# Two transformer blocks on one core: matmuls of the up stretches in program order, and the Strassen forms placed behind the norm

## Chip, core and metric

The kernel runs on one core of one Trainium2 chip. The metric is the device time of one execution in microseconds. TensorE is the matrix engine (PE in the profile, PEld its weight loads), VectorE is DVE, ScalarE is ACT, GpSimd is POOL, SyncE is SP, which issues the loads of the weights.

## What is computed

Two blocks of two layers each, in float32, width 1024. The change lies in the second block: 512 tokens and 16 learned ones (528, and 512 in the last stage), and in each of its two layers twice a gated feed-forward net, before and after a mixer.

```python
def swiglu(x, w_gate, w_up, w_down):
    return (jax.nn.silu(x @ w_gate) * (x @ w_up)) @ w_down
...
    for l in range(DEPTH):
        h = h + 0.5 * swiglu(rmsnorm(h, norm_gains[l, 0]),
                             ffn_w_gate[l, 0], ffn_w_up[l, 0], ffn_w_down[l, 0])
        h = h + mixer(rmsnorm(h, norm_gains[l, 1]), w_in[l], ...)
        h = h + 0.5 * swiglu(rmsnorm(h, norm_gains[l, 2]),
                             ffn_w_gate[l, 1], ffn_w_up[l, 1], ffn_w_down[l, 1])
    return rmsnorm(h, final_norm)[:, N_META:]
```

w_gate and w_up are 1024 x 2816, w_down is 2816 x 1024. So the net is run four times, as the stages (0,0), (0,1), (1,0) and (1,1) of layer and place.

## The kernel before

Activations lie with the features on the partitions, as 8 chunks (NK) of 128 features by 528 tokens, `xt`. Every operand of a matmul is split into a high and a low part of a faster float format, and every product is made of three matmuls (high by high, high by low, low by high): `mm3` does so for a chunk of 128 features, in two halves of the tokens, and lines 235 and 243 issue its matmuls. Weights are loaded as raw tiles by SyncE (6 buffers), split by ScalarE into `whi` (line 212) and by VectorE into `wlo` (line 213), 9 buffers each. Activations are split by `xsplit` (lines 286, 287) and `split` (lines 220, 221).

**The feed-forward stage, `ffn2`.** The hidden features are 22 blocks m of 128. For each, gate and up are computed, then `act` makes silu(gate) * up and splits it for the down matmuls. Two ways lead to gate and up. Blocks 0, 3, 7, 11, 15, 18 and 21 (DIRECT) use `group`: 8 chunks by 3 by 2 matmuls for gate and for up each. The others, 13 in stage (0,0) and 15 in each of the others, use `strassen`: the 2 x 2 product of (gate, up) weight halves and token halves in seven products instead of eight. Before blocks 8 and 16 and at the end (ROUNDS) the blocks so far go through `down`, which adds into `xt`.

**The seven products.** `pair` loads the four quarter weights a, b, c, d of a block and makes the sums s1 to s4 from them on VectorE (line 1022). Each product (`prod`) is 12 matmuls at line 1042, of 264 columns (256 in the last stage). Y and X are two halves of one PSUM tile `yx`, Z lies in another, `z`; the pool P has three such tiles. In `strassen`:

- a: Y = a x1; then ScalarE copies Y to `fg` (line 1060)
- b: X = b x2; VectorE adds X to `fg` (line 1058), first yield
- s2: Y += s2 f2; ScalarE copies Y (line 1065), second yield
- s1: Z = s1 f1; s3: Y += s3 f1; ScalarE copies Y to `fu` (line 1071), VectorE adds Z, third yield
- d: Y += d f2, and the multiplications by the norm's factors, fourth yield
- s4: Z += s4 x2, and `act`

`ffn2` interleaves two blocks: a, b of block m; d of m-1; s2 of m; s4 of m-1; s1 and s3 of m. A block's d and s4 that are left when a direct block comes are written behind its first group of matmuls.

**The forms.** f1 and f2 are sums and differences of the halves of the activations, scaled by the norm's gains but not by its root. `form` makes one of the four pairs of chunks: a scaled copy on ScalarE (line 322), four operations on VectorE (lines 319 and 325), and two splits (lines 220, 221). `finish`, called for each chunk k when the stage before has finished it, does `xsplit`, the squares for the norm (`sumsq`, lines 299, 300), and for k of 4 and over one form. The first block's last stage (`out1`) does the same for all four in its own loop ahead of stage (0,0).

**The norm.** `stats` sums squares over partitions on TensorE (ssq, line 336), and the reciprocal root is a chain of small VectorE operations (`rsqrt`, lines 357 to 375); `stats2` broadcasts it with matmuls (bc, line 388) and ScalarE copies it to `rbc` (line 411). In `group` with an r, `stats2` is written after the chunk MID (4) of 8. Block 0 then scales gate and up (`mul_r`, line 417), applies silu (line 1111), multiplies (line 1112), and splits. In stage (0,0) the first five groups (gate and up of block 0, 1 and the gate of block 2) run before the norm's factors are known: their results wait in `gur` tiles (line 1105), the last in PSUM, and `rbc` comes out of the last of these groups.

**What sets the order.** The order of the instructions on each engine is found at compile time, by a planner that lets a free engine take the first instruction of the program's order whose inputs it counts as ready; the chip then runs each engine's queue in that order. The tiles of `slot` come from one pool of 62. The down stretches and the groups of blocks over 0 already stand in the program's order; the stretches of seven products do not, nor does `ending`, which finishes the last chunk of the whole kernel in two halves with norm and output.

Of the kernel before, what the change touches and what calls it, by code (L numbers as in the profile page):

```python
# [22 lines left out]
NX = 512  # L23
NMETA = 16
T2 = NX + NMETA
NK = 8
# [34 lines left out]
class Net:  # L61
    def __init__(self, ctx, tc, d):
        nc = self.nc = tc.nc
        self.tc = tc
        self.d = d
        self.n = 0
        self.xp = ctx.enter_context(tc.tile_pool(name="xp", bufs=1))
        self.cp = ctx.enter_context(tc.tile_pool(name="cp", bufs=1))
        self.sp = ctx.enter_context(tc.tile_pool(name="sp", bufs=NSLOT))
        self.mp = ctx.enter_context(tc.tile_pool(name="mp", bufs=24))  # L70
        self.qp = ctx.enter_context(tc.tile_pool(name="qp", bufs=8))
        self.wp = ctx.enter_context(tc.tile_pool(name="wp", bufs=4))
        self.pstack = ctx.enter_context(ExitStack())
        self.block = 0
        self.filler = iter(())
        self.got = {}
        self.forms = None

        self.cst = self.cp.tile([128, 144], F32, name="cst")
        self.v2 = self.cp.tile([128, 2 * V2 + 8], F32, name="v2")  # L80
        self.v1 = self.slot("v1")
        self.xt = [self.xp.tile([128, T2], F32, name=f"xt{k}") for k in range(NK)]
        nc.scalar.dma_start(self.v1[:, : 2 * V1], d["vec1"])
        nc.gpsimd.dma_start(self.cst, d["cst"])
        nc.scalar.dma_start(self.v2, d["vec2"])
        self.pre = []
        self.ident = self.cst[:, 0:128]
        self.c1024 = self.cst[:, 128:129]
        self.c128 = self.cst[:, 129:130]
        self.hm64 = self.cst[:, 130:132]  # L90
# [124 lines left out]
    def split(self, a, name):  # L215
# [5 lines left out]
        nc.vector.tensor_tensor(out=l[:, :T], in0=a, in1=h[:, :T], op=ALU.subtract)  # L221
        return h, l

    def mm3(self, ps, w, wc, xs, T, first, last, M=128, halves=(0, 1)):


        nc = self.nc
        wh, wl = w
        xh, xl = xs
        whole = T == NX and len(halves) == 2  # L230
        for i, (a, b) in enumerate(((wh, xh), (wh, xl), (wl, xh))):
            st, sp = first and i == 0, last and i == 2
            lh = self.wcol(a, wc, M)
            if whole:
                nc.tensor.matmul(ps[:M, :], lhsT=lh, rhs=b[:, :NX], start=st, stop=sp)  # L235
                continue
            for h in halves:
                c = slice(0, 256) if h == 0 else slice(256, T)
                if T == NX:
                    o = ps[:M, c]  # L240
                else:
                    o = ps[:M, 0, 256:512] if h == 0 else ps[:M, 1, 0 : T - 256]
                nc.tensor.matmul(o, lhsT=lh, rhs=b[:, c], start=st, stop=sp)  # L243

    def outs(self, n, T, name="g", tag=None):

# [55 lines left out]
    def finish(self, k, T, g):  # L302

        c = slice(0, T)
        r = self.xsplit(k, g(k), c)
        self.sumsq(k, self.xt[k][:, c], c)
        if self.forms is not None and k >= NK // 2:
            self.form(k - NK // 2, T, g)
        return r

# [136 lines left out]
    def out1(self, srcs, ks, ins, ys, gcol, next_g, tn):  # L447


        nc = self.nc  # L450
        m0 = NK - len(srcs)
        ws = [[self.wload(s) for s in src] for src in srcs]
        ps = [[self.A("oh") for _ in srcs] for _ in range(2)]
        H = (slice(0, 256), slice(256, NX))
        rb = self.slot("rbp")
        for hf in range(2):
            c = H[hf]
            bl = (2 * hf, 2 * hf + 1)
            for i in range(len(srcs)):
                for n, (wi, col, k) in enumerate(ks):  # L460
                    self.mm3(
                        ps[hf][i], ws[i][wi], col, ins[k], NX, n == 0, n == len(ks) - 1, halves=(hf,)
                    )
                if hf == 0:
                    ys.append(self.slot("y"))
                self.evac_y(m0 + i, ps[hf][i][:, c], c, gcol, ys[m0 + i])
            pss = self.S("ssy")
            self.compact(self.acc, bl, self.c1024, pss)
            r = self.rsqrt(pss, bl, 1)
            bc = self.S("bcy")  # L470
            self.bcast(r, bl, bc)
            nc.scalar.copy(rb[:, c], bc[:, c])
        for hf in range(2):
            c = H[hf]
            cn = slice(256, tn) if hf else c
            if hf == 0:
                xs = []
            for k in range(NK):
                nc.vector.tensor_tensor(out=ys[k][:, c], in0=ys[k][:, c], in1=rb[:, c], op=ALU.mult)
                nc.vector.tensor_tensor(out=self.xt[k][:, c], in0=self.xt[k][:, c], in1=ys[k][:, c], op=ALU.add)  # L480
                if hf == 0:
                    xs.append((self.slot("xh", F32R), self.slot("xl", F32R)))
                self.xsplit(k, next_g(k), cn, xs[k])
                if hf == 1 and self.forms is not None and k >= NK // 2:
                    self.form(k - NK // 2, tn, next_g)
            for k in range(NK):
                self.sumsq(k, self.xt[k][:, cn], cn)
        return xs
# [548 lines left out]
    def prod(self, o, w, xs, c, first):  # L1037

        for k in range(NK // 2):
            l = slice(128 * k, 128 * k + 128)  # L1040
            for i, (a, b) in enumerate(((0, 0), (0, 1), (1, 0))):
                self.nc.tensor.matmul(  # L1042
                    o, lhsT=w[a][:, l], rhs=xs[k][b][:, c], start=first and k == 0 and i == 0,
                    stop=k == NK // 2 - 1 and i == 2, skip_group_check=not first,
                )
# [34 lines left out]
        act(s, u, True)  # L1080
        yield

    def ffn2(self, l, f, xs, next_g, out=None):
        nc, d = self.nc, self.d
        T = NX if (l, f) == (L - 1, 1) else T2
        self.psum(2)
# [33 lines left out]
        def ahead(m):  # L1120

            if m not in wp and seven(m):
                wp[m] = self.pair(srcs[2 * m], srcs[2 * m + 1])

        for m in range(NF):
            ahead(m)
            if seven(m):
                if seven(m + 1) and m + 1 not in ROUNDS:
                    ahead(m + 1)
# [7 lines left out]
            else:  # L1137
                ps = done[2 * m : 2 * m + 2]
                o = 2 * m + len(ps)
                if m == 0 and not ps:  # L1140
                    ps = self.outs(2, T, "gu")
                    r = self.stats(T)
                    rb = self.group(srcs[:2], xs, T, ps, r=r)
                    ps = [p[1] for p in ps]
                for i in range(o, 2 * m + 2):
                    if len(ps) == 2:
# [7 lines left out]
            if m + 1 in ROUNDS:  # L1154
# [16 lines left out]
                if fin and out is not None:  # L1171
                    self.ending(out, self.wload(dsrc(NK - 1)), acts)
                acts.clear()
        return new

    def ending(self, out, ws, acts):
# [554 lines left out]
def tile_model(ctx: ExitStack, tc: tile.TileContext, d, out, stages=ALL):  # L1731
# [18 lines left out]
    for i, s in enumerate(stages):  # L1750
# [16 lines left out]
        elif s[0] == "m2":  # L1767
            xs = net.mixer2(s[1], xs, ng)
        else:
            end = nx[0] == "end"  # L1770
            xs = net.ffn2(s[1], s[2], xs, ng, out if end else None)
            if end:
                break

# [178 lines left out]
```

## Time and profile before

| | us |
|---|---|
| median of 3 runs | 3674.74 (3673.05 to 3675.29) |
| profiled execution, time | 3672.45 |
| profiled execution, span of the trace | 3670.7 |
| TensorE busy | 3543.5 (97%) |
| VectorE busy | 2412.7 (66%) |
| ScalarE busy | 1715.2 (47%) |
| DMA, mean of the 16 engines | 82 GB/s read from and written to memory |

The profiled execution is 2.3 us shorter than the median of the runs, and 1.75 us of its time lie outside the span. The mean granted clock of TensorE was 0.988 of full. In the rows below, the idle time in brackets is that of the engine just before the instruction, with what ended it.

### The profile page before, as it was taken

To read this page: it belongs to the slowest core of one execution; us is meant where nothing else is said; L and a number is where in the kernel's file an instruction comes from. 1 tells how busy PE (TensorE), PEld (TensorE's weight loads), DVE (VectorE), ACT (ScalarE), POOL (GpSimd) and SP (SyncE) were. 2 spreads that over 40 slices of the span, in tenths; PEclk is the share of its full clock that TensorE was granted. 3 is DMA by queue.
4 is the path that set the end of the run, shared out by engine and by line. 5 is a ranking of instruction groups with operands and counts; after the bars stand their busy time and mean duration, and the time that the engine had idled before them with its cause. 6 is when DMAs were issued, how large, how long until landed. Compare 5 with 4: busy or idle time off the path is not lost. (4 is left out here: it accounts for less than half of the span.)

```text
span 3670.7 us, 60668 instructions
## 1 busy us (share of the span) xinstructions
PE 3543.5 (97%) x23303; PEld 3142.0 (86%) x23303; DVE 2412.7 (66%) x4863; ACT 1715.2 (47%) x3219; POOL 44.4 (1%) x184
## 2 busy tenths in 40 slices
PE   8999999999999799999999999998999999999998
PEld 6778888768888799998988999998999987778887
DVE  6778754787864666576546766577666664677765
ACT  3655433365543443344573443354334557444433
POOL 1000000000000000000000000000000000000000
PEclk9999999999999999999999999999999999999999
DMA  4213333212333222331121232333333212223232
GB/s 144 67 50 109 95 93 111 72 50 84 95 94 92 77 81 86 88 105 60 54 62 53 78 100 85 91 89 90 88 95 95 74 56 62 67 78 101 87 100 68
DMA packets 170178, 305.02 MB, mean 83 GB/s; under 512 B 19460, under 2 KB 29732, under 8 KB 169888
## 3 DMA queue, kind: packets, MB, share of 16 engines
q1 hardware_dynamic: 165888, 292.89, 27.1%
q0 software_dynamic: 2560, 6.93, 0.6%
q8 instruction: 183, 3.00, 0.4%
q10 hardware_dynamic: 1440, 1.32, 0.1%
q14 instruction: 107, 0.88, 0.1%
HBM read 298.97 MB, written 2.10 MB: 82 GB/s over the span
## 5 line engine op out<-in xcount | busy, mean ns | idle before, releaser
L212 ACT ACTIVATE whi<-raw 128x512 fp32r<-128x512 f32 (+1 forms) x1078 | 662.8, 619 | 1132.1 <-PE dn L235 187.5
L213 DVE TENSOR_TENSOR wlo<-raw,whi 128x512 fp32r<-128x512 f32 (+1 forms) x1078 | 722.8, 672 | 465.4 <-ACT whi L212 450.6
L235 PE MATMUL up<-xh,wlo 128*128 128x512 f32 x640 | 252.7, 395 | 0.0
L235 PE MATMUL up<-xh,whi 128*128 128x512 f32 x640 | 252.5, 395 | 0.0
L235 PE MATMUL up<-xl,whi 128*128 128x512 f32 x640 | 252.1, 394 | 0.0
L212 ACT ACTIVATE whi<-sum 128x512 fp32r<-128x512 f32 x232 | 145.5, 631 | 216.1 <-PE yx L1042 59.5
L243 PE MATMUL dn<-fah,wlo 128*128 128x256 f32 (+1 forms) x1068 | 218.0, 284 | 0.0
L243 PE MATMUL dn<-fah,whi 128*128 128x256 f32 (+1 forms) x1068 | 217.7, 284 | 0.0
L243 PE MATMUL dn<-fal,whi 128*128 128x256 f32 (+1 forms) x1068 | 217.7, 284 | 0.0
L213 DVE TENSOR_TENSOR wlo<-sum,whi 128x512 fp32r<-128x512 f32 x232 | 158.9, 688 | 57.3 <-ACT whi L212 54.0
L243 PE MATMUL g<-xh,whi 128*128 128x256 f32 (+1 forms) x848 | 185.5, 297 | 2.7 <-ACT ptm L1410 1.5
L243 PE MATMUL g<-xl,whi 128*128 128x256 f32 (+1 forms) x848 | 179.7, 288 | 0.0
L243 PE MATMUL g<-xh,wlo 128*128 128x256 f32 (+1 forms) x848 | 177.9, 287 | 0.0
L243 PE MATMUL gu<-xh,whi 128*128 128x256 f32 (+1 forms) x736 | 154.3, 290 | 14.4 <-ACT gur L1105 12.3
L243 PEld LDWEIGHTS dn<-fah,whi 128*128 128x128 f32 x1068 | 167.7, 188 | 0.0
L243 PEld LDWEIGHTS dn<-fah,wlo 128*128 128x128 f32 x1068 | 167.6, 188 | 0.0
L243 PEld LDWEIGHTS dn<-fal,whi 128*128 128x128 f32 x1068 | 167.5, 188 | 0.0
L1042 PE MATMUL yx<-fvh,whi 128*128 128x264 f32 (+1 forms) x464 | 138.7, 299 | 21.8 <-ACT fu L1071 20.1
L243 PE MATMUL gu<-xl,whi 128*128 128x256 f32 (+1 forms) x736 | 155.9, 288 | 1.2 <-DVE xl L287 1.2
L243 PE MATMUL gu<-xh,wlo 128*128 128x256 f32 (+1 forms) x736 | 155.3, 288 | 0.0
L235 PE MATMUL g<-xh,whi 128*128 128x512 f32 x344 | 146.3, 425 | 7.4 <-ACT xh L286 6.3
L243 PEld LDWEIGHTS g<-xh,whi 128*128 128x128 f32 (+1 forms) x848 | 132.8, 188 | 14.5 <-issue 7.1
(538 smaller groups left out, 9574.2 us busy)
## 6 DMA issues: line engine op xcount, KB each, us to landing
raw<-w_in SPq DMA_DIRECT2D x186, 256.0 KB, 2.8
raw<-w_up SPq DMA_DIRECT2D x176, 256.0 KB, 2.8
raw<-ffn_g SPq DMA_DIRECT2D x176, 256.0 KB, 2.8
raw<-ffn_u SPq DMA_DIRECT2D x176, 256.0 KB, 2.9
raw<-ffn_d SPq DMA_DIRECT2D x160, 256.0 KB, 2.7
raw<-w_down SPq DMA_DIRECT2D x80, 256.0 KB, 2.7
raw<-w_out SPq DMA_DIRECT2D x64, 256.0 KB, 2.7
raw<-w_pab SPq DMA_DIRECT2D x32, 256.0 KB, 2.7
```

The lines of the kernel that those rows point to most:

```text
L212: self.nc.scalar.activation(hi[:, c], raw[:, c], AF.Copy)
L213: self.nc.vector.tensor_tensor(out=lo[:, c], in0=raw[:, c], in1=hi[:, c], op=ALU.subtract)
L235: nc.tensor.matmul(ps[:M, :], lhsT=lh, rhs=b[:, :NX], start=st, stop=sp)
L243: nc.tensor.matmul(o, lhsT=lh, rhs=b[:, c], start=st, stop=sp)
L1042: self.nc.tensor.matmul(o, lhsT=w[a][:, l], rhs=xs[k][b][:, c], start=first and k == 0 and i == 0, stop=k == NK // 2 - 1 and i == 2, skip_ ...
```

## The change

It has two parts.

- A helper `mm` issues a matmul and, while `self.pinned` is set, tells the planner to keep it behind the TensorE instruction written before it (an order on the engine's own queue, no wait on a semaphore). `prod` and `mm3` use it. `pinned` is set in `ffn2` from block 1 to the end of the stage, so seven products, groups, down rounds and `ending` stand in the program's order; block 0 and the other stages do not.
- The last of the four forms (k = 7) is no longer made in `finish`, and `out1` makes none. `ffn2` makes those that are missing, in a function `forms`: in stage (0,0) all four behind the five first groups, ahead of the block loop; in the others the last one behind the group of block 0, whose `stats2` comes before it, and ahead of block 0's `act`. `ffn2` gets the norm's gains `g` for that.

```diff
--- before.py
+++ after.py
@@ -75,6 +75,7 @@
         self.filler = iter(())
         self.got = {}
         self.forms = None
+        self.pinned = False
 
         self.cst = self.cp.tile([128, 144], F32, name="cst")
         self.v2 = self.cp.tile([128, 2 * V2 + 8], F32, name="v2")
@@ -221,10 +222,15 @@
         nc.vector.tensor_tensor(out=l[:, :T], in0=a, in1=h[:, :T], op=ALU.subtract)
         return h, l
 
+    def mm(self, *a, **k):
+
+        i = self.nc.tensor.matmul(*a, **k)
+        if self.pinned:
+            self.tc.keep_in_program_order(i)
+
     def mm3(self, ps, w, wc, xs, T, first, last, M=128, halves=(0, 1)):
 
 
-        nc = self.nc
         wh, wl = w
         xh, xl = xs
         whole = T == NX and len(halves) == 2
@@ -232,7 +238,7 @@
             st, sp = first and i == 0, last and i == 2
             lh = self.wcol(a, wc, M)
             if whole:
-                nc.tensor.matmul(ps[:M, :], lhsT=lh, rhs=b[:, :NX], start=st, stop=sp)
+                self.mm(ps[:M, :], lhsT=lh, rhs=b[:, :NX], start=st, stop=sp)
                 continue
             for h in halves:
                 c = slice(0, 256) if h == 0 else slice(256, T)
@@ -240,7 +246,7 @@
                     o = ps[:M, c]
                 else:
                     o = ps[:M, 0, 256:512] if h == 0 else ps[:M, 1, 0 : T - 256]
-                nc.tensor.matmul(o, lhsT=lh, rhs=b[:, c], start=st, stop=sp)
+                self.mm(o, lhsT=lh, rhs=b[:, c], start=st, stop=sp)
 
     def outs(self, n, T, name="g", tag=None):
 
@@ -304,7 +310,7 @@
         c = slice(0, T)
         r = self.xsplit(k, g(k), c)
         self.sumsq(k, self.xt[k][:, c], c)
-        if self.forms is not None and k >= NK // 2:
+        if self.forms is not None and NK // 2 <= k < NK - 1:
             self.form(k - NK // 2, T, g)
         return r
 
@@ -481,8 +487,6 @@
                 if hf == 0:
                     xs.append((self.slot("xh", F32R), self.slot("xl", F32R)))
                 self.xsplit(k, next_g(k), cn, xs[k])
-                if hf == 1 and self.forms is not None and k >= NK // 2:
-                    self.form(k - NK // 2, tn, next_g)
             for k in range(NK):
                 self.sumsq(k, self.xt[k][:, cn], cn)
         return xs
@@ -1039,7 +1043,7 @@
         for k in range(NK // 2):
             l = slice(128 * k, 128 * k + 128)
             for i, (a, b) in enumerate(((0, 0), (0, 1), (1, 0))):
-                self.nc.tensor.matmul(
+                self.mm(
                     o, lhsT=w[a][:, l], rhs=xs[k][b][:, c], start=first and k == 0 and i == 0,
                     stop=k == NK // 2 - 1 and i == 2, skip_group_check=not first,
                 )
@@ -1080,7 +1084,7 @@
         act(s, u, True)
         yield
 
-    def ffn2(self, l, f, xs, next_g, out=None):
+    def ffn2(self, l, f, xs, g, next_g, out=None):
         nc, d = self.nc, self.d
         T = NX if (l, f) == (L - 1, 1) else T2
         self.psum(2)
@@ -1122,8 +1126,15 @@
             if m not in wp and seven(m):
                 wp[m] = self.pair(srcs[2 * m], srcs[2 * m + 1])
 
+        def forms():
+            for k in range(len(self.forms), NK // 2):
+                self.form(k, T, g)
+
+        if done:
+            forms()
         for m in range(NF):
             ahead(m)
+            self.pinned = m > 0
             if seven(m):
                 if seven(m + 1) and m + 1 not in ROUNDS:
                     ahead(m + 1)
@@ -1141,6 +1152,7 @@
                     ps = self.outs(2, T, "gu")
                     r = self.stats(T)
                     rb = self.group(srcs[:2], xs, T, ps, r=r)
+                    forms()
                     ps = [p[1] for p in ps]
                 for i in range(o, 2 * m + 2):
                     if len(ps) == 2:
@@ -1171,6 +1183,7 @@
                 if fin and out is not None:
                     self.ending(out, self.wload(dsrc(NK - 1)), acts)
                 acts.clear()
+        self.pinned = False
         return new
 
     def ending(self, out, ws, acts):
@@ -1768,7 +1781,7 @@
             xs = net.mixer2(s[1], xs, ng)
         else:
             end = nx[0] == "end"
-            xs = net.ffn2(s[1], s[2], xs, ng, out if end else None)
+            xs = net.ffn2(s[1], s[2], xs, g_of["f2"](*s[1:]), ng, out if end else None)
             if end:
                 break
```

## Rows read from the trace of the kernel before

**Rows 1.** Busy time of TensorE, the page's first part: busy us, share, instructions.
```profile
PE 3543.5 (97%) x23303; PEld 3142.0 (86%) x23303; DVE 2412.7 (66%) x4863; ACT 1715.2 (47%) x3219; POOL 44.4 (1%) x184
```

**Rows 2.** TensorE's waits: engine, tile, line <- releaser: us, times, longest us.
```profile
PE yx L1042 <- ACT fu L1071: 20.1, 35, 0.9
PE yx L1042 <- ACT fg L1065: 14.9, 15, 1.0
...
PE bc L388 <- DVE rs_y L375: 12.0, 6, 5.1
...
PE z L1042 <- DVE fg L417: 4.1, 3, 1.7
...
PE yx L1042 <- ACT fg L1060: 1.8, 2, 0.9
```

**Rows 3.** Timeline of TensorE: start us, us, engine, line, tiles, [idle before <-releaser].
```profile
2110.89 0.39 PE L1042 MATMUL yx<-xh,whi 128*128 128x264 f32 x1 [0.93 <-ACT fg L1060]
...
2113.22 0.39 PE L1042 MATMUL yx<-fvh,whi 128*128 128x264 f32 x1 [0.59 <-DVE fg L1058]
```

**Rows 4.** The same of products s3 and d of a block.
```profile
1326.18 0.39 PE L1042 MATMUL yx<-fuh,whi 128*128 128x264 f32 x1 [1.02 <-ACT fg L1065]
1326.40 0.28 PE L1042 MATMUL yx<-ful,whi 128*128 128x264 f32 x1
...
1327.62 0.28 PE L1042 MATMUL yx<-fuh,wlo 128*128 128x264 f32 x1
1328.77 0.39 PE L1042 MATMUL yx<-fvh,whi 128*128 128x264 f32 x1 [0.87 <-ACT fu L1071]
```

**Rows 5.** Timeline of ScalarE between these two products.
```profile
1327.82 0.63 ACT L212 ACTIVATE whi<-raw 128x512 fp32r<-128x512 f32 x1 [1.69 <-PE yx L1042]
1328.36 0.36 ACT L1071 COPY fu<-yx 128x264 f32<-128x264 f32 x1
```

**Rows 6.** Timeline of ScalarE around the norm ahead of the third such stage.
```profile
2482.25 0.63 ACT L220 ACTIVATE fvh<-tv 128x528 fp32r<-128x528 f32 x1
2482.79 0.73 ACT L286 ACTIVATE xh<-xt,v 128x528 fp32r<-128x528 f32 x1
...
2499.86 0.65 ACT L220 ACTIVATE fah<-fg 128x528 fp32r<-128x528 f32 x1 [0.79 <-DVE fg L1112]
...
2501.88 0.36 ACT L1060 COPY fg<-yx 128x264 f32<-128x264 f32 x1
```

**Rows 7.** Windows, matmuls of line 1042: stretch, us, PE and PEld busy (count), clock.
```profile
1317.50:1348.60 31.10, 28.99 (x228) 28.07 (x228) 1.00 0.32 93
...
1547.20:1566.20 19.00, 18.45 (x144) 17.75 (x144) 1.00 0.28 94
...
sum 522.90, PE 492.79 PEld 474.67; mean PE 24.64 PEld 23.73
```

**Rows 8.** Lines by shape, 1257 to 1282 us: busy us, mean ns, idle.
```profile
L319 DVE SCALAR_TENSOR_TENSOR tv<-xt,v,tu 128x264 f32<-128x264 f32 x4 | 2.0, 489 | 0.0
...
L221 DVE TENSOR_TENSOR fvl<-tv,fvh 128x528 fp32r<-128x528 f32 x4 | 2.8, 702 | 0.0
```

**Rows 9.** Timeline of TensorE at the third such stage's norm.
```profile
2489.41 0.28 PE L1042 MATMUL yx<-xh,wlo 128*128 128x264 f32 x1
2494.84 2.61 PE L388 MATMUL bc<-cst,rs_y 128*128 128x128 f32 x10 [5.14 <-DVE rs_y L375]
```

**Rows 10.** Timeline of TensorE at the first such stage's norm.
```profile
1281.32 0.81 PE L243 MATMUL gu<-xh,whi 128*128 128x256 f32 x2 [12.28 <-ACT gur L1105]
```

**Rows 11.** Windows around it: us, then busy us (count) by engine, clock.
```profile
1257.00:1269.00 12.00, 9.27 (x63) 8.05 (x63) 12.00 (x30) 7.92 (x16) 0.00 (x0) 1.00 0.01 2
...
1281.30:1297.00 15.70, 14.38 (x89) 14.05 (x90) 5.87 (x19) 3.34 (x6) 0.00 (x0) 0.71 0.13 39
```

**Rows 12.** Timeline of VectorE behind that norm.
```profile
1306.82 0.70 DVE L417 TENSOR_TENSOR fg<-gu,rbc 128x528 f32<-128x528 f32 x1
...
1311.90 0.71 DVE L417 TENSOR_TENSOR fg<-gu,rbc 128x528 f32<-128x528 f32 x1 [0.55 <-PE gu L243]
```

## The prediction

> **What bounds the kernel now.** I read the page first, then the waits of TensorE, then the timeline of single places. TensorE is busy 3543.5 of 3670.7 us [rows 1], so only 127 us of the span are open to any gain, and an edit that makes TensorE wait where it worked before costs its full length. The waits [rows 2] show which idle time this change can reach: 20.1 us before products that wait for the copy of line 1071 (35 times), 14.9 us for the copy of line 1065 (15 times), 12.0 us for the reciprocal root ahead of the norm's broadcast, 4.1 us behind the first scaled gate tile of line 417. The copy of line 1060, the one between a block's first and second product, is waited for only twice, 1.8 us in all. There are 58 blocks with seven products, so 56 times something lay between. I call a block's products by the weight they use: a, b, s2, s1, s3, d, s4, in the order in which the program writes them; d and s4 are written behind b and s2 of the following block.
>
> **Part 1, the pinned order: the steady stretches.** Today each engine's instructions are put in order at compile time, first ready first. So between a and b of a block stand products that are ready: s1 of the same block, pieces of d of the block before, pieces of a of the next. Pinned, b stands right behind a. b writes another half of the same PSUM tile that the copy of line 1060 reads, and the trace shows that it does wait for that copy: at 2110.89 us, where nothing else was ready, TensorE stood 0.93 us until line 1060 had ended [rows 3]. So pinning opens this hole in every block.
>
> Its size: matmuls of a product start 0.122 us apart ((1327.62 - 1326.40) / 10 [rows 4]), a product of 12 is 1.46 us. From s3 at 1326.18 to d at 1328.77, with the copy of line 1071 between, are 2.59 us [rows 4], so a wait for such a copy costs 2.59 - 1.46 = 1.13 us. Why so long for a copy of 0.36 us: ScalarE first splits a weight tile that the same product has released (0.63 us from 1327.82), and the copy starts at 1328.36 [rows 5]. Product a releases a weight tile too, so I take 1.13 for b. In the first block of a group that follows a direct block the split of that block's activation (0.65 us, line 220 in rows 6) stands in front as well: 1.13 + 0.55 = 1.7. A group's first s2 has no d before it and waits for the addition of line 1058: 2113.22 - 2110.89 = 2.33, less 1.46, is 0.87 [rows 3]. All other waits vanish: a and b of the next block stand between s3 and d, s1 between s2 and s3.
>
> The sum per stage has five groups beyond the first blocks: two of three blocks behind a direct block (1.7 + 2 x 1.13 + 0.87 = 4.8 each), one of three behind a down round (4.3), one of two behind a direct block (3.7), one of two behind a down round (3.1): 20.7, four stages 83. Today the same 20 stretches take 522.9 us; twelve have 228 matmuls and eight 144, 3888 in all [rows 7]. At 0.122 us, and 0.118 in the last stage, where a product has 256 columns for 264, they need 469 to 471, so 52 to 54 us are lost now. **Net +30 us.** The lower bound is +7: if the copy goes ahead of the weight's split, the hole shrinks to what the split does not add, 0.45 for 0.87, and b costs 0.7 (58 x 0.43 = 25 less). The upper bound is +45, if each d or s3 also loses some of its cover.
>
> Here the Trainium skill speaks against the change, "TensorE: Matmul & The Clock Gate", section "Step-by-step: what each phase is for": the engine may pull weight loads ahead, but matmuls stay in the program's order. The trace agrees, since b's wait of 0.93 us stood while later matmuls were in the queue. By that rule nothing on the chip refills a hole that the pinned order leaves.
>
> **Part 2, the forms behind the norm: three later boundaries.** The last form (one of four) leaves the chain between the last activation chunk and the norm's root. It costs ScalarE one small operation and two splits, VectorE four small operations of 0.49 and two low splits of 0.70 [rows 8]; 2.7 to 2.9 us of VectorE's stand between the operations of the root. Without them the root may come 2.4 us sooner.
>
> But where do they go? They need no norm; their tiles come from one pool, though, and the trace speaks for the pool serving tiles in the program's order: at 2482.79 the split of chunk 7 starts just as the last split of form 2, written before it, is out; and the copy of block 1 (line 1060) starts at 2501.88, behind the split of block 0 of 2499.86 [rows 6], though the last matmul of its product started at 2489.41 [rows 9]. So I take it that the form's tiles come behind the tile of the broadcast, and block 0's activation behind the form's. From the end of the broadcast (2494.84 + 2.61 [rows 9]) the path to b of block 1 is then: broadcast copy 0.7; five small operations, taken at 0.49 each, 2.45; 0.16 for the split of 0.65 that stands beside the last of them; two low splits 1.4; gate and up scaled 1.4; their product 0.7; the activation's split 0.65; copy 0.36: 7.8 us, all idle on TensorE since the order is pinned. Then 0.87 before s2 and 1.13 before the next b. Today's waits there are 5.14 at the broadcast [rows 9], 1.4 behind it (4.1 over three boundaries [rows 2]), 0.5 and twice 0.86: 8.8. After: 5.14 - 2.4 + 7.8 + 0.87 + 1.13 = 12.5. That is +3.7 for this boundary; the others have the same chain with shorter waits at the broadcast, and I take +3.5 for each, **+10 us** for three. Bounds: -2.4 each (-7) if the tiles don't bind, since the form then runs beside the root; +6 each if the clock stays low longer.
>
> **Part 3, the first boundary.** Here all four forms leave the stretch in front of the norm. TensorE stands there 12.28 us at one place [rows 10] and 2.7 and 1.3 more around it (12.00 less 9.27 busy, 15.70 less 14.38 [rows 11]), and works behind it at a mean granted clock of 0.71 [rows 11], so that some 4.5 us are lost to the half clock besides: 21 us. Most of it is VectorE and ScalarE busy with forms, and goes. Behind the norm four forms stand in front of the activations of blocks 0, 1 and 2: 4.0 to 4.5 us each, since in a form one small operation waits for the other, 16 to 18 in all. The scaling of block 2 frees a PSUM tile; today it is read at 1306.82 to 1307.5, and the group that needs a third tile starts at 1311.9, where the one before it ends [rows 12]. So 4.4 us of the 18 are covered and 13.6 are a new wait, with a slow clock behind it again (4.5): -21 + 18 = -3, and I take **-2**. Bounds: -17 if the tiles don't bind, +5 if the forms are stretched by weight splits between them.
>
> **Part 4, the ending.** The second half's 18 matmuls of the last block stood before the first half's sums and broadcast and now come behind them: 18 x 0.12 = 2.2 us at most, nothing if the root hides them; I take +1. The DMAs of weights are issued by SyncE in the order in which weight tiles come free; that order isn't pinned and the tiles' use is the same, so I cost it at nothing. If a load came late, a wait in the down stretches would show it.
>
> **Sum** against the profiled 3672.45 us: 30 + 10 - 2 + 1 = +39, 3711.5; the median of the runs stands 2.3 above the profiled one: **3714 us**.
>
> **Rivals.**
> - *Holes are harmless* (faster): b need not wait, or weight splits come later than the copy, so that pinning only removes the waits of lines 1065 and 1071. Only the first-s2 waits stay (20 x 0.87 = 17 for 53): 3672.5 - 36 - 7 - 2 = 3628, with the offset 3630. It stands against the two waits of 0.9 us. It decides the sign where b's wait costs under 0.46 us for 1.13 (39 / 58 = 0.67 less).
> - *The pool does not bind*: forms run where VectorE is idle. Steady +30, first boundary -17, others -7, end +1: +7, 3682. For it: 62 tiles, never all in use as far as I count; against it: rows 6.
> - *Copy first*: the steady term is +7 for +30: 3691. Against it: rows 5, where the split goes first.
> - *The clock falls*: holes of 1 us in every block might lower the clock; each drop would cost some 3.4 us (7 us at half), 20 stretches 68 us: 3782. Against it: a clock of 1.00 in all 20 stretches today, with waits of 0.9 us in them [rows 7]. This is the mechanism of the Trainium skill's "TensorE: Matmul & The Clock Gate", section "A second HAM failure mode: psum-queue depth-cycling", where short idle times between groups of matmuls make the clock oscillate; in the rows here the trace doesn't agree.
> - *The pin changes nothing*: the order stays and only the forms move: 3682.
>
> **How the numbers follow.** Forecast 0.62, harmless holes 0.13, pool 0.09, copy first 0.09, clock 0.03, nothing changed 0.04. A measurement of this kernel tells about 0.2%, 7.3 us. Below 3667: the harmless holes and a bit of the pool's case, 0.15. Within 0.2%: most of the pool's case and the unchanged order, 0.10. The rest, 0.75, is slower. The range takes in the pool's case and copy first at its lower end and +45 with +18 at its upper end (3672.5 + 2.3 + 57): 3674 to 3732; outside are harmless holes and the clock.
>
> **What would show it.** Right: some 50 waits before products for line 1060, 0.8 to 1.4 us each, and nearly none for lines 1065 and 1071; the 20 stretches together some 550 us; a single wait of 6 us or more between the broadcast and b of block 1 in the three later boundaries; in the first stage the 12.28 us gone and some 14 us behind the norm. Wrong: if b stands behind a without a gap, part 1 falls and with it the sign; if the forms' operations stand beside the root or the group of block 0, part 2 and 3 fall; if the clock in the stretches is below 1.00, the sum is too small.

## The result and the profile after

| | before | after |
|---|---|---|
| median of 4 runs, us | 3673.89 (3671.39 to 3675.29) | 3716.78 (3711.89 to 3718.47) |
| span of the profiled execution, us | 3670.7 | 3716.7 |
| TensorE busy, us | 3543.5 | 3544.7 |

After over before is 1.0115 (95% interval 1.0098 to 1.0133): 43 us slower by the medians, where +39 was forecast for the profiled execution and 3714 us for the median. The profiled execution of the changed kernel is the slowest of its four, so the spans differ by 46.0 us. TensorE does the same work in the same busy time; what came in is idle time. In the changed kernel every matmul of this part is issued at line 227 (the helper), and lines have moved: 1060, 1058, 1065, 1071, 417, 388 are now 1064, 1062, 1069, 1075, 423, 394.

TensorE's waits, the view of [rows 2] (engine, tile, line <- releaser: us, times, longest us):

```profile
PE yx L227 <- ACT fg L1064: 81.5, 58, 8.0
PE yx L227 <- DVE fg L1062: 13.7, 23, 0.6
PE gu L227 <- DVE fg L423: 12.1, 1, 12.1
...
PE bc L394 <- DVE rs_y L381: 7.3, 4, 2.8
```

The copies of lines 1069 and 1075, 35 us before [rows 2], are waited for no more at all. The copy behind product a is waited for in each of the 58 blocks, 81.5 us for 1.8. The three longest of these waits stand at the later boundaries (6.64, 7.33 and 7.96 us); the other 55, of 0.91 to 1.72 us each, come to 60 us.

The windows over the same 20 steady stretches, the view of [rows 7], here with all engines (stretch, us, busy us and count of PE, PEld, DVE, ACT and POOL, granted clock, DMA share, GB/s):

```profile
1404.50:1436.80 32.30, 28.91 (x231) 28.07 (x230) 24.21 (x42) 15.91 (x30) 0.00 (x0) 1.00 0.29 87
...
3627.30:3651.10 23.80, 20.58 (x146) 19.87 (x144) 13.96 (x24) 10.24 (x21) 0.00 (x0) 0.86 0.21 59
sum 560.20, PE 491.51 PEld 476.36 DVE 404.15 ACT 275.31 POOL 0.00; mean PE 24.58 PEld 23.82 DVE 20.21 ACT 13.77 POOL 0.00
```

They take 560.2 us for 522.9 [rows 7]. The last stretch is the only one with a clock under 1.00.

A steady group, TensorE's waits in the timeline (start us, us, instruction, [idle before <-releaser]), where 1407.01 is b of the group's first block, 1409.33 its s2 and 1416.37 b of the second:

```profile
1407.01 0.39 PE L227 MATMUL yx<-xh,whi 128*128 128x264 f32 x1 [0.91 <-ACT fg L1064]
...
1409.33 0.39 PE L227 MATMUL yx<-fvh,whi 128*128 128x264 f32 x1 [0.59 <-DVE fg L1062]
...
1416.37 0.39 PE L227 MATMUL yx<-xh,whi 128*128 128x264 f32 x1 [0.92 <-ACT fg L1064]
```

and ScalarE ahead of that last b:

```profile
1415.42 0.63 ACT L213 ACTIVATE whi<-raw 128x512 fp32r<-128x512 f32 x1 [0.56 <-ACT fu L1075]
1415.95 0.36 ACT L1064 COPY fg<-yx 128x264 f32<-128x264 f32 x1
```

This is the picture of [rows 4, 5] at another product: the weight's split of 0.63 us goes first, the copy of 0.36 us behind it, and TensorE stands 0.92 us.

The third such stage's norm, TensorE, as in [rows 9]:

```profile
2511.31 1.54 PE L394 MATMUL bc<-cst,rs_y 128*128 128x128 f32 x10 [2.81 <-DVE rs_y L381]
2520.17 0.59 PE L227 MATMUL yx<-xh,whi 128*128 128x264 f32 x1 [7.33 <-ACT fg L1064]
...
2523.78 0.59 PE L227 MATMUL yx<-fvh,whi 128*128 128x264 f32 x1 [0.60 <-DVE fg L1062]
```

and ScalarE:

```profile
2512.50 0.66 ACT L417 COPY rbc<-bc 128x512 f32<-128x512 f32 x2 [2.85 <-PE bc L394]
2513.05 0.53 ACT L328 ACTIVATE tt<-xt,v 128x264 f32<-128x264 f32 x1
...
2519.21 0.64 ACT L221 ACTIVATE fah<-fg 128x528 fp32r<-128x528 f32 x1 [0.79 <-DVE fg L1116]
2519.76 0.36 ACT L1064 COPY fg<-yx 128x264 f32<-128x264 f32 x1
```

The root comes earlier, a wait of 2.81 us for 5.14 [rows 9]. Then the last form starts 0.55 us after the broadcast's copy, block 0's activation is split at 2519.21, and only then comes the copy of line 1064: 7.33 us of wait for b.

The first boundary, TensorE, as in [rows 10]:

```profile
1301.74 0.78 PE L227 MATMUL gu<-xh,whi 128*128 128x256 f32 x2 [12.08 <-DVE fg L423]
```

ScalarE there, with the broadcast's copy and the first operation of the first form behind it:

```profile
1275.38 0.66 ACT L417 COPY rbc<-bc 128x512 f32<-128x512 f32 x2 [1.29 <-PE bc L394]
1275.93 0.53 ACT L328 ACTIVATE tt<-xt,v 128x264 f32<-128x264 f32 x1
```

and VectorE's scaling of block 2, which frees the PSUM tile, as in [rows 12]:

```profile
1300.89 0.70 DVE L423 TENSOR_TENSOR fg<-gu,rbc 128x528 f32<-128x528 f32 x1
```

The wait of 12.28 us in front of the norm is gone, and one of 12.08 us stands behind it.

For the sums below all traces are divided at the same instructions: the seven-product stretches beyond block 3 with the pieces of d and s4 behind the direct groups (from TensorE's first start to that of the next group); the three later boundaries (from the first matmul of block 0 to that of block 3); and the first boundary (from its first matmul to the first product of block 4). All in us; the median is over the runs, the other columns are from the profiled execution.

| | median | stretches | later boundaries | first boundary |
|---|---|---|---|---|
| before | 3673.9 | 591.0 | 124.4 | 74.3 |
| after | 3716.8 | 630.2 | 136.1 | 67.0 |
| pin alone | 3715.4 | 627.2 | 129.2 | 73.7 |
| forms alone | 3667.8 | 591.2 | 124.0 | 67.1 |
| d between a and b | 3683.4 | 599.3 | 129.6 | 66.8 |
| root in its own tile | 3703.9 | 625.9 | 128.9 | 64.7 |
| copy first | 3690.8 | 607.4 | 129.1 | 66.6 |
| covered order | 3613.0 | 568.4 | 100.6 | 61.5 |
| covered order, no pin | 3622.8 | 578.1 | 100.8 | 61.3 |

So the 46 us between the two profiled executions are +39 in the stretches, +12 at the later boundaries, -7 at the first, and some 2 us elsewhere. Not all of it is waiting: at the later boundaries TensorE's waits rise from 21 to 30 us, and the other 3 us are matmuls that run slower, more of them at the half clock, behind the longer waits.

### The profile page after: what moved, and what is told of

Same layout as the page of the kernel before. It is cut to its first block, busy times and chain, and to the rows that moved or that the text cites. A ratio compares the mean times of both kernels' runs of the same rounds, so it can differ in the third digit from the quotient of the medians.

```text
span 3716.7 us, 60666 instructions
## 1 busy us (share of the span) xinstructions
PE 3544.7 (95%) x23303; PEld 3146.8 (85%) x23303; DVE 2423.9 (65%) x4863; ACT 1720.5 (46%) x3219; POOL 44.3 (1%) x184
## 5 line engine op out<-in xcount | busy, mean ns | idle before, releaser
L227 PE MATMUL g<-xh,whi 128*128 128x256 f32 (+4 forms) x1192 | 332.2, 335 | 9.8 <-ACT xh L292 5.9
L227 PE MATMUL g<-xl,whi 128*128 128x256 f32 (+4 forms) x1192 | 318.0, 321 | 0.3 <-DVE xl L293 0.3
L227 PE MATMUL g<-xh,wlo 128*128 128x256 f32 (+4 forms) x1192 | 314.4, 319 | 0.0
L227 PE MATMUL up<-xh,wlo 128*128 128x512 f32 (+1 forms) x768 | 289.3, 377 | 0.0
L227 PE MATMUL up<-xl,whi 128*128 128x512 f32 (+1 forms) x768 | 289.0, 377 | 0.1
L227 PE MATMUL up<-xh,whi 128*128 128x512 f32 (+1 forms) x768 | 288.3, 377 | 0.0
L227 PE MATMUL yx<-xh,whi 128*128 128x264 f32 (+1 forms) x464 | 139.3, 300 | 81.5 <-ACT fg L1064 81.5
L227 PEld LDWEIGHTS g<-xl,whi 128*128 128x128 f32 (+1 forms) x1192 | 200.6, 188 | 15.5 <-issue 2.6
L227 PEld LDWEIGHTS g<-xh,wlo 128*128 128x128 f32 (+1 forms) x1192 | 199.9, 188 | 14.9
L227 PE MATMUL gu<-xh,whi 128*128 128x256 f32 (+2 forms) x848 | 197.7, 302 | 14.6 <-DVE fg L423 12.1
L214 DVE TENSOR_TENSOR wlo<-sum,whi 128x512 fp32r<-128x512 f32 x232 | 159.8, 689 | 71.8 <-ACT whi L213 66.8
L227 PE MATMUL gu<-xl,whi 128*128 128x256 f32 (+2 forms) x848 | 198.2, 301 | 0.7 <-DVE xl L293 0.7
```

The source lines that it names most:

```text
L214: self.nc.vector.tensor_tensor(out=lo[:, c], in0=raw[:, c], in1=hi[:, c], op=ALU.subtract)
L227: i = self.nc.tensor.matmul(*a, **k)
```

## The experiments

The theory was that of the prediction: the pin opens a hole between a and b, as long as one copy behind one weight split; the forms cost little by themselves, and at the boundaries they come late because the pool gives out its tiles in the program's order. The rivals: the forms carry the loss; the pin as such is bad; the hole is only the first of several waits; the hole is a fixed path and not a queue.

**Pin alone.** The forms go back to where they were.

```diff
-        if self.forms is not None and NK // 2 <= k < NK - 1:
+        if self.forms is not None and k >= NK // 2:
             self.form(k - NK // 2, T, g)
...
                 self.xsplit(k, next_g(k), cn, xs[k])
+                if hf == 1 and self.forms is not None and k >= NK // 2:
+                    self.form(k - NK // 2, tn, next_g)
```

> The changed kernel with the forms made where they were made before, so that only the pinned order is left. Theory (the pinned order opens a hole between products a and b of every block; the forms' place is a second, smaller matter): the 20 steady stretches stay as long as in the changed kernel, 39 us over before; at the three later boundaries the wait of b falls from 7.3 us to about 3.3, but the wait for the root comes back to what it was (some 2.4 us more); the first boundary is as before. Some 3674 + 39 + 5 = 3718 us. Rival (the moved forms are what makes the kernel slow, the order costs little): at most 3690.

Measured: 3715.4 us, 1.0108 of before (1.0093 to 1.0123). The third stage's norm, TensorE:

```profile
2517.24 2.61 PE L394 MATMUL bc<-cst,rs_y 128*128 128x128 f32 x10 [5.12 <-DVE rs_y L381]
2523.22 0.59 PE L227 MATMUL yx<-xh,whi 128*128 128x264 f32 x1 [3.37 <-ACT fg L1066]
```

The wait for the root is back at 5.12 us, and b's wait is 3.37 for 7.33. The pin alone makes +42 us over before; the rival that put the loss on the forms falls.

**Forms alone.** The pin is left out.

```diff
-            self.pinned = m > 0
```

> The changed kernel without the pin; only the forms' new place is left. Theory: the 20 steady stretches go back to their 522.9 us; the first boundary keeps its gain of some 7 us; the three later ones lose 1 to 2 us each, as a piece of s1 now fills part of the wait: 3670 to 3674 us. Rival (the forms carry the loss): 3690 or more.

Measured: 3667.8 us, 0.9985 of before (0.9976 to 0.9994). TensorE's waits:

```profile
PE yx L227 <- ACT fu L1075: 19.8, 35, 0.9
PE yx L227 <- ACT fg L1069: 14.0, 14, 1.0
PE z L227 <- DVE fg L423: 12.2, 3, 4.9
```

The waits for the copies of d and s3 are back (before: 20.1 and 14.9 us [rows 2]) and the stretches are at 591.2 us. The first boundary keeps its 7 us. At the later ones the shorter wait for the root is paid back by the wait for block 0's scaling: 12.2 us, 4.1 before [rows 2]. The run is 2 us below what was expected, and a small gain by itself.

The parts do not add up: 41.7 - 5.9 = 36 for the measured 43. In the profiles the 7 us that are missing stand at the later boundaries: 136.1 with both, 129.2 with the pin alone and 124.0 with the forms alone, for 124.4 before. Some 5 of them are waits: without the pin, s1 of block 1 fills a part of the wait that the form makes; with it, nothing does. The other 2 to 3 are slower matmuls, with more of them at the half clock.

**d between a and b.** One exchange in the written order, pin and forms as in the changed kernel.

```diff
         nc.scalar.copy(s[:, a], Y)
+        yield
         self.prod(X, w["b"], x2, a, True)
...
                 next(cur)
                 next(pend, None)
                 next(cur)
                 next(pend, None)
                 next(cur)
+                next(cur)
                 pend = cur
```

> The changed kernel with one exchange in the program's order: product d of the block before now stands between a and b of a block, s4 of it between b and s2 (before: a b d s2 s4). The pin stays. Theory (the loss is the missing cover between a and b, not the pin): b's wait vanishes in the 35 blocks that follow another one, 35 x 1.15 = 40 us, and stays in the 23 first blocks of a group: about 3677 us. Rival (b's wait is only the first of several: d then waits for the copy of line 1075 or s2 for the addition): 3695 or more.

Measured: 3683.4 us, 1.0023 of before (1.0014 to 1.0033): 33 us less than the changed kernel for one exchange in the order. The waits for the copy behind a:

```profile
PE yx L227 <- ACT fg L1064: 48.9, 23, 8.0
```

23 are left for 58, one in each first block of a group, as expected, and 32.6 us of waiting are gone; no wait for the copy of line 1075 came up, so that rival falls. It is 6 us above the expectation, and windows over three stretches of two blocks behind a direct block show a part of it (columns as above):

```profile
1578.50:1602.30 23.80, 21.08 (x147) 20.35 (x146) 14.92 (x26) 11.05 (x21) 0.00 (x0) 0.86 0.23 66
...
2810.20:2830.70 20.50, 18.28 (x145) 17.66 (x145) 14.73 (x25) 10.76 (x21) 0.00 (x0) 1.00 0.25 71
```

Two of the four stretches of that kind (the other at 2412.9, clock 0.85) ran at a lower mean clock and took 3 us more than their twin. Their waits for b were 2.12 and 1.81 us, the twin's 1.63.

**The root in its own tile.** The broadcast root leaves the pool of 62, so that nothing ahead of the forms in the pool waits for it.

```diff
-NSLOT = 62
+NSLOT = 61
...
-        rb = self.slot("rbc")
+        rb = self.fp.tile([128, T2], F32, tag="f", name=self.nm("rbc"))
```

> The changed kernel with the broadcast root in a tile of its own, taken out of the pool of 62 (61 are left). Theory (the pool serves its tiles in the program's order, so that the forms' tiles stand behind the broadcast's): the forms now start before the broadcast, b's wait at the three later boundaries falls from 7.3 us to about 3.4, the root comes up to 2 us later, and most of the 12 us in the first boundary goes: 3692 to 3702 us. Rival (the forms come late because the planner ranks them behind, whatever the tiles): as the changed kernel, 3717.

Measured: 3703.9 us, 1.0080 of before (1.0064 to 1.0097). ScalarE at the first boundary:

```profile
1269.60 0.58 ACT L1110 COPY gur<-gu 128x528 f32<-128x528 f32 x1
1270.08 0.52 ACT L329 ACTIVATE tt<-xt,v 128x264 f32<-128x264 f32 x1
...
1273.98 0.63 ACT L418 COPY rbc<-bc 128x512 f32<-128x512 f32 x2
```

The form's first operation now starts 3.9 us ahead of the broadcast's copy, where it came 0.55 us behind it. At the third stage's norm TensorE shows

```profile
2503.90 2.51 PE L395 MATMUL bc<-cst,rs_y 128*128 128x128 f32 x10 [3.55 <-DVE rs_y L382]
2509.78 0.59 PE L228 MATMUL yx<-xh,whi 128*128 128x264 f32 x1 [3.37 <-ACT fg L1065]
```

that is 3.37 us for 7.33, with a root 0.74 us later (3.55 for 2.81). Nothing else was edited, so it was the root's tile in the common pool that held the forms back; that the pool serves its tiles strictly in the program's order is the reading that fits, and was not tried otherwise. The total gain is 13 us, 2 us short of what was expected: the wait in the first boundary fell only from 12.08 to 9.1 us. There the scaling of block 0 still starts behind all four forms, at 1288.32, 14 us after the start of the broadcast's copy. Whether its tiles or VectorE's order hold it was not separated.

**Copy first.** The copy is put ahead of the weight's split on ScalarE.

```diff
-            for i, (a, b) in enumerate(((0, 0), (0, 1), (1, 0))):
+            for i, (a, b) in enumerate(((1, 0), (0, 0), (0, 1))):
...
-                if seven(m + 1) and m + 1 not in ROUNDS:
-                    ahead(m + 1)
                 cur = self.strassen(wp.pop(m), xs, T, rb, act)
                 next(cur)
+                if seven(m + 1) and m + 1 not in ROUNDS:
+                    ahead(m + 1)
```

> The changed kernel with two edits that let the copy of line 1064 (1060 in the kernel before) stand ahead of the weight's split on ScalarE: the three matmuls of a chunk go low by high first, so that a high weight tile is in use until the product's last matmul, and the next block's weights are prepared behind the first copy in the program's order. Theory (the hole is 0.36 us of copy behind a split of 0.63 us): the wait of b in the steady stretches falls from 0.92 to some 0.45 us, 58 x 0.45 = 26 us less, about 3691. Rival (the hole is the path from TensorE to ScalarE and back, whatever stands in its queue): 3712 to 3717.

Measured: 3690.8 us, 1.0046 of before (1.0031 to 1.0061). ScalarE and TensorE at the block of which the changed kernel's rows stand above:

```profile
1415.68 0.38 ACT L1064 COPY fg<-yx 128x264 f32<-128x264 f32 x1 [0.51 <-PE yx L227]
1415.95 0.64 ACT L213 ACTIVATE whi<-raw 128x512 fp32r<-128x512 f32 x1
```

```profile
1416.11 0.39 PE L227 MATMUL yx<-xh,wlo 128*128 128x264 f32 x1 [0.47 <-ACT fg L1064]
```

The copy starts without the split ahead of it, and the hole is 0.47 us for 0.92. So half of it was the queue on ScalarE, the other half the copy with its way there and back. The rival of a fixed path falls. The first blocks behind a direct block keep their 1.6 us, since the activation's split still goes first there. That the total fell by the expected 26 us is in part luck: the waits for the copy give 18.8 of them (81.5 to 62.7), and most of the rest is clock, in the last stretch (20.4 us for 23.8) and at the later boundaries, whose waits are only 2 us shorter. This was also a rival of the prediction (3691 us), made true by two edits, and it meets that total by other terms: +16 in the stretches for +7, +5 at the later boundaries for +10, and -8 at the first for -2.

**A covered order.** If the pin costs only what its order leaves open, an order with a product behind each copy of the steady part must beat both kernels. `strassen` now returns its products one by one, and `ffn2` writes them so:

```diff
+                if prev is None:
+                    go(cur, "a")
+                    if m == 1:
+                        go(cur, "b s2")
+                        run(late)
+                        go(cur, "s1 s3")
+                        full = False
+                    else:
+                        run(late)
+                        go(cur, "s1 b")
+                        full = True
+                elif full:
+                    go(cur, "a")
+                    go(prev, "s2")
+                    go(cur, "b")
+                    go(prev, "s3")
+                    go(cur, "s2")
+                    go(prev, "d s4")
+                    go(cur, "s1 s3")
+                    full = False
+                else:
+                    go(cur, "a")
+                    go(prev, "d")
+                    go(cur, "b")
+                    go(prev, "s4")
+                    go(cur, "s2 s1 s3")
```

`late` holds the activation of a direct block, which is so written behind the next block's a; the root's tile of its own is kept. In the first stage the forms are written behind the activations of blocks 0 and 1.

> The changed kernel with the pin, but with an order of products in which each copy has a product behind it. First blocks of a group: a, s1, b, then a of the next block, s2, b of the next, s3, s2 of the next, d, s4; later ones a, d of the one before, b, s4 of the one before, s2, s1, s3. A direct block's activation is written behind the next block's a, the broadcast root has a tile of its own, and in the first stage the forms are written behind the activations of blocks 0 and 1. Theory (the pin costs only what its order leaves uncovered): the 20 steady stretches lose less than 10 us for 53 before, the first boundary gains 7 to 15, the later ones are a few us shorter than before: 3605 to 3630 us. Rival (new waits take the place of the old ones, or the clock falls more often): 3660 or more.

> The kernel of the run with the covered order, without the pin. Theory (the planner, which takes the first ready instruction, opens the waits for lines 1065 and 1071 of the kernel before by taking products out of turn): 10 to 40 us slower than the pinned one. Rival (the written order alone is what matters): within 5 us of the pinned one.

In these two kernels the activations of blocks 7 and 15 were written behind the down rounds that need them, so those rounds leave them out and pair the others with the weights of the wrong blocks: the kernels compute something else. They took 3704.8 us and 3718.7 us, and the waits of the first show what that cost:

```profile
PE dn L229 <- DVE xt L1222: 49.1, 56, 1.3
```

A block whose scaling is not yet written keeps its PSUM tiles, and the down round had one tile for three: 49 us of waits, 56 of them. That says nothing for or against the theory, but it prices two of three PSUM tiles that stay taken. With the activation ahead of the round, and the forms of the first stage spread over three places:

```diff
-                if not seven(m + 1):
+                if not seven(m + 1) or m + 1 in ROUNDS:
                     run(late)
...
-            if done and m == FORMS_AT:
-                forms()
+            if done and m in FORMS_AT:
+                forms(FORMS_AT[m])
...
-FORMS_AT = 2
+FORMS_AT = {1: 1, 2: 2, 3: 4}
```

> The covered order of products with the pin, where a direct block's activation is written ahead of a down round if one follows, so that no PSUM tile stays taken through the round; in the first stage one form each is written behind the activations of blocks 0 and 1 and two behind that of block 2. Theory (the pin costs only what its order leaves uncovered): steady stretches 10 us under before, the three later boundaries 25 us, the first one 7 to 13: 3622 to 3635 us. Rival (something else takes the place of the waits): 3660 or more.

Measured: 3613.0 us, 0.9835 of before (0.9821 to 0.9848): 63 us faster than the runs of the kernel before that were taken beside it (3675.6 us), and 104 us faster than the changed kernel, with the same pin. Its waits (lines moved once more: 1059 is the additions, 425 the scaling of direct blocks):

```profile
PE yx L229 <- DVE fg L1059: 8.9, 13, 0.9
...
PE z L229 <- DVE fg L425: 8.0, 12, 2.3
...
PE gu L229 <- DVE fg L425: 5.7, 1, 5.7
```

and its 20 steady stretches:

```profile
1531.10:1548.70 17.60, 17.60 (x147) 17.60 (x146) 13.12 (x23) 9.56 (x18) 0.00 (x0) 1.00 0.32 98
...
sum 499.90, PE 482.42 PEld 473.52 DVE 416.96 ACT 287.00 POOL 0.00; mean PE 24.12 PEld 23.68 DVE 20.85 ACT 14.35 POOL 0.00
```

The largest are now 8.9 us for the additions and 8.0 and 5.7 us for the scaling of direct blocks; of waits for a copy, 1.9 us behind a and 1.3 us behind s3 are left. The stretches take 499.9 us for 522.9; the one shown has TensorE busy in all of its 17.6 us. The later boundaries fell from 124.4 to 100.6 us and the first one from 74.3 to 61.5. At the third stage's norm, b of block 1 now goes ahead of the broadcast, where it stood behind block 0's activation:

```profile
2461.88 0.39 PE L229 MATMUL yx<-xh,whi 128*128 128x264 f32 x1 [1.00 <-ACT fg L1067]
...
2464.42 1.48 PE L396 MATMUL bc<-cst,rs_y 128*128 128x128 f32 x10 [0.82 <-DVE rs_y L383]
```

Of the 24 us at the later boundaries 17 are waits (21.2 before, 4.5 now). Most of the other 7 is clock: before, some 6 us were lost there by matmuls at the half clock; here the clock stays at 1.00 in all three. The run is 9 us below the expected range: the boundaries gave what was expected (-24 and -13), the stretches 23 for the 10 that the first of the two kernels above had led me to expect.

> The same kernel without the pin. Theory (the planner takes products out of turn and opens the waits of b and d again): 8 to 25 us slower than the pinned one. Rival (the written order alone matters): within 5 us of it.

Measured: 3622.8 us, 0.9864 of before (0.9850 to 0.9877), 10 us slower than with the pin. Its waits:

```profile
PE yx L229 <- ACT fg L1067: 23.0, 25, 1.0
```

The copy behind a is waited for 25 times again, 23.0 us (with the pin twice, 1.9 us). So the planner takes b out of the written order to a place where the copy is not yet done; why it counts it as done there was not looked into. The pin is worth 10 us on top of the rest, all of them in the stretches (578.1 to 568.4). Without it this kernel is still some 50 us faster than before: 13 in the stretches, where the order is what was changed, and 24 and 13 at the boundaries, where the order, the later activations, the root's tile and the forms' places were changed together and not separated.

## Why the prediction was right

**The hole between a and b, the sign of it all.** Right: 55 waits of 0.9 to 1.7 us outside the norms, and none for the copies that d and s3 waited for. The two waits of [rows 3] had shown that b depends on the copy, and [rows 4, 5] its size: 0.87 there, 0.92 measured. The experiment with d between a and b shows that the missing cover is the cause: 35 of 58 waits went and 33 us with them. It also shows what [rows 3] could not, where the product behind b, s2, had to wait for b's own addition: d of the block before was ready, since it goes into that place without a wait, and in the changed kernel it stood behind b's 0.92 us all the same.

**The size of the steady term**: +30 was forecast, +37 came in the 20 stretches (+39 with the pieces behind the direct groups). The term that was too small is the first block of a group: a wait of 0.87 + 0.55 = 1.42 was set for its b behind a direct block, and it is 1.45 to 1.72 us. The third b of a group waits 0.96 to 1.09 where I took the ordinary 0.87, since the split of an activation stands in ScalarE's queue too (0.65 us from 1426.10 on, ahead of the weight's split and the copy at 1427.44), and the last stretch lost some 3 us to the clock. The Trainium skill, "TensorE: Matmul & The Clock Gate", section "A second HAM failure mode: psum-queue depth-cycling", tells of a kernel in which TensorE idles shortly between groups of matmuls so often that its clock goes back and forth between the two levels. Here the clock fell in one stretch of 20 and stayed at 1.00 in the other 19, with waits of 0.9 to 1.6 us for every b, so as a rival for the whole it was rightly given little.

**The later boundaries**: +10 forecast, all of it waits; +11.7 measured (5.4, 4.2 and 2.1), of which 8.5 are waits and the rest matmuls that run slower behind them, for which the sum has no term, only its upper bound. In the stage that was worked out, 7.8 us was set for the path from the broadcast to b, 7.33 measured. The wait for the root was set at 5.14 - 2.4 = 2.7, measured 2.81. The step that I had only inferred, that the root's tile in the pool holds the form back, is shown by the root's own tile.

**The first boundary**: -2 forecast, -7 measured. The waits came as forecast: 16.3 us in all before and 12.8 after, with the new one at 12.08 where 13.6 was set. The term that was mis-sized is the clock, which the sum takes as the same 4.5 us on both sides. Behind the wait some 3 us are lost (a mean clock of 0.64 over the 8.3 us from 1301.7), and the sum has nothing for the start of this stretch, where 3 us were lost before and none after. The windows of its first 7 us, before and then after:

```profile
1243.00:1250.00 7.00, 7.00 (x35) 6.91 (x36) 5.76 (x21) 2.26 (x6) 0.00 (x0) 0.55 0.52 150
1243.00:1250.00 7.00, 6.81 (x54) 6.58 (x55) 6.35 (x23) 3.34 (x11) 0.00 (x0) 1.00 0.46 150
```

Why the clock differs there was not tried.

**The ending**: +1 forecast, 0.6 measured. The loads of weights, costed at nothing, show no new wait.

The errors are +7 to +9 on the stretches, +2, -5 and nothing, and partly cancel: the total was off by 4 us by the medians and by 7 by the profiled executions, the terms by more. That the number came so close is in part luck; the sign and the place of the loss are not. What the prediction did not single out is that the two parts work against each other: it costed the boundaries with both at once, and 7 us of the +12 are their meeting.

**Two sums that do not come out.** The upper end of the range is given as +45 with +18, which is 63; the 57 used is 39 and 18, so that the terms named would give 3738 us for 3732. The lower bound of +7 for the stretches does not follow from 58 times 0.43 us, which leaves +5, but from the 52 blocks outside the first groups. The measured time lies inside the range either way.

## What to carry to other kernels

Before an order is pinned, go through it link by link: behind each product that is read out and then written beside, count what stands between, and price an empty place with the nearest wait of the same shape in the trace, with what else stands in the copying engine's queue. In this case pinning paid only with an order that has cover at the steady links: the same pin cost 42 us in one order and gave 10 in another. And an instruction that is ready can be held by the pool its tile comes from: take the tile that waits out of the shared pool, or write the waiting work later.

## What was not expected of the hardware

The clock fell in a stretch whose waits were 1.72 and 0.59 us, with a product of matmuls between them. TensorE in the last stretch of the changed kernel:

```profile
3632.99 0.58 PE L227 MATMUL yx<-fvh,whi 128*128 128x256 f32 x1 [0.59 <-DVE fg L1062]
3633.37 0.41 PE L227 MATMUL yx<-fvl,whi 128*128 128x256 f32 x1
3633.58 0.41 PE L227 MATMUL yx<-fvh,wlo 128*128 128x256 f32 x1
...
3639.07 0.28 PE L227 MATMUL yx<-ful,whi 128*128 128x256 f32 x1
3639.19 0.28 PE L227 MATMUL yx<-fuh,wlo 128*128 128x256 f32 x1
```

Matmuls start 0.21 us apart from 3633.37 on and 0.12 us apart from 3639.07 on. The granted clock is 0.50 from 3633.2 to 3639.0 (1.2 GHz) and 1.00 (2.4 GHz) behind it; the mean of the stretch is 0.86. Other stretches with a wait of 1.6 and one of 0.6 us kept a clock of 1.00 (1582.5 to 1603.9). With the pin alone the same stretch has waits of 1.44 and 0.59 us, stays at 1.00 and takes 20.8 us for 23.8. In the kernel with d between a and b, waits of 2.12 and 1.81 us, each followed by one of 0.59, stand in the two stretches with a lowered clock (0.86 and 0.85). What decides it was not tried.
